# Seven products instead of eight in the Fourier half of an output projection: an encoder layer on one Trainium2 core

## The chip, the cores and the metric

The program runs on one core of one Trainium2 chip. The metric is the device time of the whole program in microseconds (us); before the change the median of three runs is 958.73 us (958.66 to 958.79). All inputs are float32 in HBM and the result is written back to HBM. In the profile PE is TensorE (matmuls and transposes), PEld its weight loads, DVE is VectorE, ACT is ScalarE, POOL is GpSimd, and SP is SyncE, which here issues the DMAs.

## The reference

One layer is applied to a prompt of 256 tokens and a sample of 2048 tokens, width 1024. Cut to what matters:

```python
def encoder_layer(x, w_in, rpb, w_fourier, b_fourier, g_pre, g_na, g_f, w_out, g_post):
    h = rms_norm(x, g_pre)
    proj = h @ w_in
    q, k, v, z_a, u_f, z_f = jnp.split(proj, [...], axis=-1)
    y_a = neighbourhood_attention(q, k, v, rpb)
    y_f = fourier_mix(u_f, w_fourier, b_fourier)
    mixed = jnp.concatenate([rms_norm(y_a, g_na) * jax.nn.silu(z_a),
                             rms_norm(y_f, g_f) * jax.nn.silu(z_f)], axis=-1)
    out = mixed @ w_out
    return x + rms_norm(out, g_post)
```

Both halves of `mixed` are 512 wide. The change concerns the second half: (y_f * silu(z_f)) of 2304 tokens x 512, times the lower 512 rows of `w_out` (512 x 1024, with the gain g_f folded in). The factor of the rms norm is one number per token and is multiplied in when the product leaves PSUM.

## The kernel before

**Stages.** Projections and the Fourier transform fill the first 590 us or so. Then come the attention steps, and at the end the attention half of the output projection (18 tiles of 128 tokens), with the last norm, the residual and the store.

**The attention loop.** There are 36 groups G[k], k = 9 * pr + i: four pairs of heads (pr), and for each the prompt (i = 0) and eight blocks of 256 sample tokens. The loop `for k in range(2, len(G) + 1)` (main loop of the attention, "step k" in this text) works on two groups at once: scores and softmax of G[k], and transposes and value product of G[k-1]. Every engine's order is the order in which the code is written. On PE a step is:

1. `scores(G[k])`: 12 matmuls (L1229, tiles `s`, four PSUM tiles: three of tag "a", which has three buffers, and one of tag "b", which has two).
2. `transp(G[k-1], 0)`: transposes of the first block's softmax weights into `ptb` (L1570). ACT copies one head's half to SBUF (`pt`), DVE the other (L1574).
3. `f_mm(k, range(6))`: six matmuls of the Fourier half (L1497, `po<-wo`, in the page also `po<-w`).
4. `transp(G[k-1], 1)`: the second block, into the same `ptb`, so after the copies of point 2.
5. `f_mm(k, range(6, 12))`: six more matmuls.
6. `pv(G[k-1])`: the value product (L1586), first with the `pt` of block 0, then with that of block 1.

Around them DVE does `bias_max` (L1251, four per step, it reads `s` and writes `w`), the `pt` copies, two reciprocals (L1260) and the product `y` with the gate (L1600). ACT does `exps` (L1256), its `pt` copies and the high part of the next q (`split_q`, L1208). POOL does `soft` (L1263, four per step: it scales the weights `w`, which PE transposes a step later), the low part of q (L1209), the sum of squares `ysq` (L1607), and in steps with i = 5 to 8 the low part of the next pair's k (`split_k`, L1141).

**The Fourier half.** A tile is 128 tokens x 512, laid out as four chunks of 128 (`raw`, loaded by `ys_load`). `ys_mul` multiplies it by the gate on POOL (L1474); `ys_split` makes a high part `yh` (ACT, L1483) and a low part `yl` (DVE, L1488), so that a float32 product becomes three fp32r matmuls per chunk: yh by high weights, yh by low weights, yl by high weights. One half of the output (512 columns) is 4 chunks x 3 = 12 matmuls; a tile has two halves and takes two steps, tile t in steps 2t and 2t + 1. `f_evac` scales a half and writes it to `ofs` (DVE for the first half, L1529; ACT for the second, L1526). The weights lie ready in SBUF as `wo1`.

**Pools and queue.** `gt` hands out 13 buffers of 4 KB per partition (weights `wo1` take eight of them). All DMAs are issued by SP in the written order; each waits for the eighth one before it.

Of the kernel before, what the change touches and what calls it, by code (L numbers as in the profile page):

```python
# [19 lines left out]
D = 1024  # L20
# [154 lines left out]
def build(tc, A, O):  # L175
# [962 lines left out]
    def split_k(kk, x, pool=False):  # L1138
        ts = slice(x * KQ, (x + 1) * KQ)
        (nc.gpsimd.tensor_copy if pool else nc.scalar.copy)(kk[0][:, ts], kk[1][:, ts].bitcast(F32))  # L1140
        nc.gpsimd.tensor_tensor(out=kk[1][:, ts], in0=kk[1][:, ts].bitcast(F32), in1=kk[0][:, ts].bitcast(F32),  # L1141
                                op=ALU.subtract)
# [63 lines left out]
    def split_q(g):  # L1206
        qh, ql = g["qh"], g["ql"]
        nc.scalar.copy(qh, ql.bitcast(F32))  # L1208
        nc.gpsimd.tensor_tensor(out=ql, in0=ql.bitcast(F32), in1=qh.bitcast(F32), op=ALU.subtract)  # L1209
# [228 lines left out]
    gpb = sm.tile([128, D], F32, name="gpb", bufs=1)  # L1438
# [24 lines left out]
    def ys_load(d):  # L1463
# [4 lines left out]
        if half:  # L1468
            d["z"] = sm.tile([128, 4, 128], F32, tag="yz", name="yz", bufs=1)
            nc.sync.dma_start(d["z"], zD[0, :, ts].rearrange("(c p) t -> p c t", p=128))  # L1470
# [5 lines left out]
    def y_parts(d):  # L1476
        d["h"] = sm.tile([128, 4, 128], F32R, tag="yh", name="yh", bufs=3)
        d["l"] = sm.tile([128, 4, 128], F32R, tag="yl", name="yl")
# [6 lines left out]
    def y_lo(d):  # L1485
        if "l" not in d:
            d["l"] = sm.tile([128, 4, 128], F32R, tag="yl", name="yl")
# [15 lines left out]
    def xt_load(d):  # L1503
        d["xt"] = gt([128, D], F32, "xt")
# [8 lines left out]
    def a_mm(d, n, js=range(12)):  # L1513
        if js[0] == 0:
            d["p", n] = ps.tile([128, 512], F32, tag="a" if n else "b", name="po", bufs=3 if n else 2)
        out_mm(d, n, js, d["p", n], lambda n, x, c: WO[x][:, c, n * 512:n * 512 + 512])
# [62 lines left out]
    def pv(g):  # L1579
# [28 lines left out]
        if R is None or hc:  # L1608
            nc.sync.dma_start(yD[0, pr, :, ts], y)

    WO = []

    WK = (24, 26, 28, 29, 31, 32, 33, 34)
    NT = {4: range(2, 4), 8: range(4, 8), 10: range(8, 12), 11: range(12, 16), 12: range(16, 18),
          32: range(4), 34: range(4, 8), 36: range(8, 12)}

# [8 lines left out]
    nc.sync.dma_start(yD[1, 3, :, TP:], Y[:, TP:])  # L1625
    f_mm(0)
# [12 lines left out]
    prep(G[4])  # L1639
    ones32 = sm.tile([128, 32], F32, name="ones32", bufs=1)  # L1640
    nc.vector.memset(ones32, 1.0)
    for k in range(2, len(G) + 1):
# [13 lines left out]
        if k == 9:  # L1656
            nc.sync.dma_start(gpb, pbc(A["gpost"]))
        if k == 23:
            wp = pt.enter_context(tc.tile_pool(name="wp", bufs=1, side="right"))
            WO.extend(wp.tile([128, 4, D], F32R, name="w0%d" % x) for x in range(2))  # L1660
        if k in WK:
            y = WK.index(k)
            nc.sync.dma_start(WO[y % 2][:, y // 2].bitcast(F32), woD[y % 2, y // 2])
        x = k // 2 + 1
        if g:
            scores(g)
            if 2 < k < 34 and k % 2 == 0:
                ys_mul(ftiles[x])
                if x + 1 < 18:
                    ys_load(ftiles[x + 1])  # L1670
            bias_max(g, 0, 0)
            exps(g, 0, 0)
            bias_max(g, 0, 1)
# [4 lines left out]
        if g:  # L1678
# [3 lines left out]
            f_mm(k, range(6))  # L1682
            soft(g, 0)
            exps(g, 1, 1)
        else:
# [3 lines left out]
        if f:  # L1689
            transp(f, 1)  # L1690
        if g:
# [4 lines left out]
            soft(g, 1)  # L1696
            if k == 2:
# [6 lines left out]
        if g:  # L1704
            f_mm(k, range(6, 12))
        else:
            a_mm(atiles[0], 1, range(6))
        if k % 2 and x < 18:
            ys_split(ftiles[x])
        if pr < 3 and i in (5, 6, 7, 8):  # L1710
            split_k(KK[pr + 1], i - 5)
        if k == 34:
            ys_split(atiles[0])
        if g:
# [3 lines left out]
        if f:  # L1718
            pv(f)
        if k + 1 in NT:  # L1720
            norm_sums(sqs if k < 31 else ysq, NT[k + 1])
        if k == 12:
            pq_.close()
        if k + 1 < len(G):
            prep_v(G[k + 1])
        if k + 3 < len(G):
            prep(G[k + 3])
        if k == 28:
            xk = [kp.tile([128, T], F32, tag=x, name="xk") for x in ("kh", "kl")]
        if 32 <= k < 36:  # L1730
            x, d = k - 32, atiles[k - 32]
            d["xt"] = xk[x // 2][:, x % 2 * D:x % 2 * D + D]
            nc.sync.dma_start(d["xt"], A["xn"][d["t"] * 128:d["t"] * 128 + 128, :])
        if k == 32:
            ys_load(atiles[0])
        if k in (34, 35):
            ys_load(atiles[k - 33])
            of_load(atiles[k - 34])

# [112 lines left out]
```

## Time and profile before

| | |
|---|---|
| time, median of three runs | 958.73 us |
| span of the profiled execution, first to last instruction | 957.4 us |
| attention steps 2 to 35 | 606.28 to 846.90 us from the span's start |
| step 36 and the output phase | 846.90 to 957.40 us |
| DVE busy | 707.8 us (74%) |
| ACT busy | 494.8 us (52%) |
| POOL busy | 435.4 us (45%) |

The profiled execution is told by its span; the time of a run has 1.3 us more around it. A busy PE in this profile is a PE with matmuls in flight: one matmul of 512 columns is shown with some 0.39 us, while the next starts 0.23 us after it. So the spacing of starts, not the shown duration, is what a matmul costs on a full PE.

### The profile page before, as it was taken

How to read it: one execution, taken by the hardware profiler on the slowest of the kernel's cores; microseconds unless marked ns; L12 is line 12 of the kernel's file. 1: busy time of each engine (PE TensorE's matmuls, PEld its weight loads, DVE VectorE, ACT ScalarE, POOL GpSimd, SP SyncE). 2: the span in 40 equal slices, each digit the busy share in tenths (PEclk: the TensorE clock that was granted, in tenths of full speed). 3: DMA queues.
4: the chain of work that ended last, by engine and by line, in shares of the span. 5: the costliest groups of instructions: out<-in, count | busy, mean ns of one | idle time of the engine just before them, and what ended most of it. 6: DMA issues, size and time to landing. Idle time of an engine off the chain costs nothing.

```text
span 957.4 us, 16751 instructions
## 1 busy us (share of the span) xinstructions
PE 949.5 (99%) x5625; PEld 790.3 (83%) x5625; DVE 707.8 (74%) x1298; ACT 494.8 (52%) x1068; POOL 435.4 (45%) x411
## 2 busy tenths in 40 slices
PE   9999999999999999999999999999999999999997
PEld 8889988888888888888888779788788888888886
DVE  6758987787975865697887369776666656659997
ACT  6735676423334532233344267677676766644443
POOL 4100002465750302575566055567678686524444
PEclk9999999999999999999999999999999999999998
DMA  9899697557758894499889997788877998989993
GB/s 357 297 383 334 245 343 264 187 193 280 296 190 331 304 342 144 175 345 356 306 297 340 335 329 247 232 241 271 262 241 239 285 301 255 287 289 346 330 346 129
DMA packets 140077, 269.80 MB, mean 282 GB/s; under 512 B 13178, under 2 KB 80464, under 8 KB 136728
## 3 DMA queue, kind: packets, MB, share of 16 engines
q1 hardware_dynamic: 139640, 268.32, 80.5%
q8 instruction: 45, 0.74, 0.3%
q10 hardware_dynamic: 288, 0.40, 0.1%
q14 instruction: 40, 0.33, 0.1%
q0 software_dynamic: 64, 0.02, 0.0%
HBM read 179.00 MB, written 96.81 MB: 288 GB/s over the span
## 4 chain that ended last, share of the span: by engine, by line
PE 98%; DVE 1%; DMA 0%; issue 0%; DVEq 0%
PE po L1497 20%; PE mm L166 18%; PE mm L164 18%; PE mm L165 18%; PE pv L1586 6%; PE ptb L1570 6%; PE s L1229 4%; PE py L164 1%; PE py L165 1%; PE py L166 1%; PE ptb L1043 1%; DMA x<-x 0%; PE pab L1053 0%; PE ppq L1096 0%; PE pz L166 0%; PE pz L164 0%
## 5 line engine op out<-in xcount | busy, mean ns | idle before, releaser
L164 PE MATMUL mm<-xh,wa 128*128 128x512 f32 x448 | 174.4, 389 | 0.0
L165 PE MATMUL mm<-xl,wa 128*128 128x512 f32 x448 | 174.3, 389 | 0.0
L166 PE MATMUL mm<-xh,wa 128*128 128x512 f32 x448 | 174.3, 389 | 0.0
L545 POOL TENSOR_TENSOR ws<-wr 128x512 f32<-128x512 f32 x16 | 23.4, 1465 | 217.8 <-DVE wa L560 127.6
L1263 POOL TENSOR_SCALAR w<-w,m 128x465 f32<-128x465 f32 (+9 forms) x136 | 84.8, 635 | 46.2 <-DVE m L1260 35.5
L166 PEld LDWEIGHTS mm<-xh,wa 128*128 128x128 f32 x448 | 84.1, 188 | 17.6
L164 PEld LDWEIGHTS mm<-xh,wa 128*128 128x128 f32 x448 | 84.1, 188 | 17.5
L165 PEld LDWEIGHTS mm<-xl,wa 128*128 128x128 f32 x448 | 84.1, 188 | 17.4
L1497 PE MATMUL po<-wo,yh 128*128 128x512 f32 x272 | 90.5, 414 | 0.0
L560 DVE TENSOR_TENSOR wa<-wr,wa 128x512 fp32r<-128x512 f32 x60 | 71.8, 1205 | 22.0 <-ACT wa L559 21.8
L1497 PE MATMUL po<-w,yh 128*128 128x512 f32 x280 | 86.8, 391 | 0.0
L1256 ACT ACTIVATE w<-w,m 128x465 f32<-128x465 f32 (+9 forms) x136 | 78.3, 579 | 13.7 <-DVE m L1251 13.3
L1251 DVE CUSTOM_DVE_ANT_1 w<-s,tb 128x465 f32<-128x465 f32 (+8 forms) x124 | 61.2, 531 | 10.1 <-PE s L1229 9.6
L165 PE MATMUL mm<-vl,xh 128*128 128x512 f32 x168 | 65.5, 390 | 0.0
L598 POOL TENSOR_TENSOR mt<-mt,rmask 128x880 f32<-128x880 f32 (+2 forms) x24 | 50.8, 2129 | 32.2 <-DVE mt L594 20.1
L164 PE MATMUL mm<-vh,xh 128*128 128x512 f32 x168 | 65.4, 389 | 0.0
L166 PE MATMUL mm<-vh,xl 128*128 128x512 f32 x168 | 65.4, 389 | 0.0
L1574 DVE COPY pt<-ptb 120x384 f32<-120x384 f32 (+5 forms) x72 | 40.5, 562 | 28.6 <-PE ptb L1570 27.8
L891 DVE TENSOR_TENSOR f<-u,mm 128x512 f32<-128x512 f32 x64 | 43.4, 679 | 24.2 <-PE mm L166 19.7
L1497 PEld LDWEIGHTS po<-w,yh 128*128 128x128 f32 x280 | 52.2, 188 | 10.9 <-issue 0.4
L1570 PE MATMUL ptb<-ident,w 128*120 128x128 f32 (+8 forms) x422 | 58.8, 276 | 0.0
L1586 PEld LDWEIGHTS pv<-pt,v 120*64 120x64 f32 (+9 forms) x880 | 47.4, 136 | 12.9 <-issue 9.7
(287 smaller groups left out, 2369.8 us busy)
## 6 DMA issues: line engine op xcount, KB each, us to landing
wr<-wz SPq DMA_DIRECT2D x48, 512.0 KB
vl<-sD SPq DMA_DIRECT2D x20, 512.0 KB
xm<-xm SPq DMA_DIRECT2D x9, 1024.0 KB
oD<-ofs SPq DMA_DIRECT2D x18, 512.0 KB
of<-oD SPq DMA_DIRECT2D x18, 512.0 KB
yr<-yD SPq DMA_DIRECT2D x34, 256.0 KB
zD<-f SPq DMA_DIRECT2D x16, 512.0 KB
xD<-nx SPq DMA_DIRECT2D x14, 512.0 KB
```

The source lines that it names most:

```text
L164: nc.tensor.matmul(out, lh, rh, start=first, stop=False)
L165: nc.tensor.matmul(out, lh, rl, start=False, stop=False)
L166: nc.tensor.matmul(out, ll, rh, start=False, stop=last)
L560: nc.vector.tensor_tensor(out=o[:, 1], in0=src, in1=o[:, 0].bitcast(F32), op=ALU.subtract)
L598: nc.gpsimd.tensor_tensor(out=o, in0=i, in1=rmask[:, m0:m0 + n].unsqueeze(2).to_broadcast([128, n, 80]), op=ALU.add)
L891: nc.vector.tensor_tensor(out=dst(f, b), in0=src(uu[u]), in1=src(p), op=op)
L1251: nc.vector.tensor_tensor_reduce(out=rows(g["w"][b][:, h, :n], w), in0=rows(g["s"][2 * b + h][:, :nr * sw(w)], sw(w))[:, :, :w], in1=tv, s ...
L1256: nc.scalar.activation(w, w, AF.Exp, bias=m[:, h:h + 1], scale=-1.0, accum_out=m[:, 2 + h:3 + h])
L1263: nc.gpsimd.tensor_scalar(w, w, m[:, 4 + h:5 + h], 1.0, ALU.mult, ALU.mult)
L1497: nc.tensor.matmul(p, (d["l"] if x == 2 else d["h"])[:, c], w(n, int(x == 1), c), start=j == 0, stop=j == 11)
L1570: nc.tensor.transpose(ptb[h][:nk, j * 128:j * 128 + 128], g["w"][b][:, h, c0:c0 + nk], ident)
L1586: nc.tensor.matmul(p[hs, b], g["v"][:nk, v, hs], g["pt"][b][:nk, h, j * 128:j * 128 + 128], start=j == 0, stop=j == len(ch) - 1)
```

## The change

Tiles 8 to 17 are taken in five pairs: pair P with tiles t and t + 1 runs in steps 2t to 2t + 3 (P["k"] = 16, 20, 24, 28, 32). With the first tile's two chunk pairs called A11, A12, the second tile's A21, A22, and the weights cut into B11, B12, B21, B22 (256 x 512 each), the eight products of a pair become seven (Strassen's scheme in Winograd's form):

- sums of the inputs: S1 = A21 + A22, S2 = S1 - A11, S3 = A11 - A21, S4 = A12 - S2
- sums of the weights, made once: T1 = B12 - B11, T2 = B22 - T1, T3 = B22 - B12, T4 = B21 - T2
- products: A11 B11, A12 B21, S2 T2, S1 T1, S3 T3, S4 B22, A22 T4

A product has two chunks, so six matmuls. `p_mm` puts two products into each of a pair's first three steps, at the places of the two `f_mm` blocks, and one into the fourth step. The products of X add up in one PSUM tile (`px`, tag "b") through all four steps; those of Z (`pz`, tag "a", as three of the score tiles) take a new tile each time.

What goes with it:

- **Input sums** (`o_sum`, four of 128 x 256 per pair, POOL), the gate product of the pair's tiles (`o_mul`, POOL), high parts (`o_hi`: two of 128 x 512 on ACT, one on DVE, one of 128 x 256 on ACT) and low parts (`o_lo`: three of 128 x 512 and one of 128 x 256, DVE). Before, a pair of tiles had two high parts (ACT) and two low parts (DVE).
- **Reading out** (`o_out`): eight per pair, two on ACT and six on DVE; before, four per two tiles, two on each.
- **Weight sums**: `t_load` in step 9 loads four pieces of 512 KB, then `t_scale` (ACT), `t_sum` (DVE and POOL), `t_hi` (ACT) and `t_lo` (DVE) run in steps 10 to 16, at the places of the table TS (step, slot). The table AT holds the places of a pair's work (step within the pair, slot).
- **q** is split two steps ahead (`split_q(G[k + 2])`, loads `prep(G[k + 4])`), before one step; in steps 17 and 26 the low part of k goes to DVE.
- The Fourier tiles' norms are taken in steps 6 to 9 (before 8, 10, 11, 12), so that the space of `sqs` can become a pool of seven buffers (`qt`) from step 8 on.
- The weights of the last phase (`WO`) lie in other buffers, `gpb` is loaded in step 34 (before 9), and `xt` of the first four tiles in step 35 and in the first output tile (before in steps 32 to 35).

The core of the diff:

```diff
-    def split_k(kk, x, pool=False):
+    def split_k(kk, x, pool=False, vec=False):
...
-        nc.gpsimd.tensor_tensor(out=kk[1][:, ts], in0=kk[1][:, ts].bitcast(F32), in1=kk[0][:, ts].bitcast(F32),
+        (nc.vector if vec else nc.gpsimd).tensor_tensor(out=kk[1][:, ts], in0=kk[1][:, ts].bitcast(F32), in1=kk[0][:, ts].bitcast(F32),
...
-    NT = {4: range(2, 4), 8: range(4, 8), 10: range(8, 12), 11: range(12, 16), 12: range(16, 18),
+    NT = {4: range(2, 4), 6: range(4, 8), 7: range(8, 12), 8: range(12, 16), 9: range(16, 18),
...
+    def t_load(j):
+        for x in range(2):
+            TR[j, x] = qt([128, D], F32, "wt")
+            nc.sync.dma_start(TR[j, x], A["wo"][1, j + 2 * x])
...
+    def t_lo(j, x, e):
+        src = TR[j, x].rearrange("p (n e) -> p n e", n=2)
+        h, l = TT[j, x]
+        if x:
+            e.tensor_tensor(out=l, in0=src, in1=f_(h), op=ALU.subtract)
+        else:
+            V.scalar_tensor_tensor(out=l[:, 0], in0=src[:, 0], scalar=-1.0, in1=f_(h[:, 0]), op0=ALU.mult,
+                                   op1=ALU.subtract)
+            V.tensor_tensor(out=l[:, 1], in0=src[:, 1], in1=f_(h[:, 1]), op=ALU.subtract)
+
+    TS = ((9, 2, t_load, 0), (9, 6, t_load, 1), (10, 4, t_scale, 0), (11, 3, t_sum, 0, 0, V),
+          (11, 7, t_sum, 0, 1, V), (11, 8, t_scale, 1), (11, 8, t_sum, 0, 2, nc.gpsimd), (12, 2, t_sum, 1, 0, V),
+          (12, 5, t_sum, 0, 3, V), (12, 7, t_sum, 1, 1, nc.gpsimd), (12, 5, t_hi, 0, 0, qt), (12, 6, t_hi, 0, 1, gt),
+          (13, 1, t_lo, 0, 0, V), (13, 4, t_sum, 1, 2, V), (13, 6, t_hi, 1, 0, gt), (13, 8, t_sum, 1, 3, V),
+          (14, 2, t_lo, 1, 0, V), (14, 5, t_lo, 0, 1, V), (14, 7, t_hi, 1, 1, qt), (16, 6, t_lo, 1, 1, V))
...
+    def product(p, a, name, first, cs=range(2)):
+        h, l = a
+        for c in cs:
+            bh, bl = B_(name)[c]
+            for i, (y, b) in enumerate(((h, bh), (h, bl), (l, bh))):
+                nc.tensor.matmul(p, y[:, c], b, start=first and c == i == 0, stop=c == 1 and i == 2,
+                                 skip_group_check=not first)
...
+    AT = (("A3", -1, 8, nc.gpsimd), ("H21", 0, 2, V), ("X2", 2, 3, V), ("M0", -3, 7, nc.gpsimd), ("L4", 2, 0, V),
+          ("X3", 3, 5, V), ("Z1", 1, 7, V), ("L3", 1, 2, V), ("A1", -1, 0, nc.gpsimd), ("X0", 0, 4, nc.scalar),
+          ("A2", -1, 7, nc.gpsimd), ("M1", -2, 8, nc.gpsimd), ("Z0", 0, 8, V), ("X1", 1, 5, nc.scalar),
+          ("L21", 0, 4, V), ("Z1b", 1, 7, V), ("H3", 0, 6, nc.scalar), ("HD", -2, 6, nc.scalar),
+          ("H4", 1, 8, nc.scalar), ("LD", -2, 7, V), ("A4", 0, 7, nc.gpsimd), ("Z2", 2, 7, V))
...
+    PROD = (("X", "D", 0, "11", True), ("Z", "D", 1, "21", True), ("X", "S21", 0, "T2", False), ("Z", "S21", 1, "T1", True),
+            ("X", "S3", 0, "T3", False), ("Z", "S4", 0, "22", True), ("X", "S3", 1, "T4", False))
+
+    def p_mm(P, s, n):
+        if 2 * s + n < 7:
+            p, a, x, b, first = PROD[2 * s + n]
+            if first:
+                P[p] = ps.tile([128, 512], F32, tag="b" if p == "X" else "a", name="p" + p.lower(), bufs=2 if p == "X" else 3)
+            product(P[p], half_of(P[a], x), b, first)
...
-            f_mm(k, range(6))
+            if k < P0:
+                f_mm(k, range(6))
+            side(k, 1)
+            pairs(k, p_mm, 0, 3, 0)
...
-            if k + 1 < len(G):
-                split_q(G[k + 1])
+            if k + 2 < len(G):
+                split_q(G[k + 2])
...
-        if g:
+        if g and k < P0:
             f_mm(k, range(6, 12))
+        elif g:
+            pairs(k, p_mm, 0, 3, 1)
```

In AT the names are: M gate product, A input sum, H high part, L low part (of D, the first tile; S21, which is S2 and S1; S3 with A22; S4), X and Z a read-out of `px` or `pz`. `side(k, slot)` puts the work of TS and AT at ten places of a step, slot 0 after the first `exps`, 1 and 2 on either side of the first `soft`, 4 after the second transposes, 5 after the second `soft`, 6 ahead of the second block of matmuls, 7 and 8 behind it, 9 after `pv`.

Three places show how the order moves. First PE, step 19, the fourth step of the first pair, from the first transposes to the value product; before:

```order
L1570 MATMUL ptb<-ident,w 80x128 x4
L1497 MATMUL po<-wo_5086,yh 128x512 x2
L1497 MATMUL po<-wo_5086,yl 128x512
L1497 MATMUL po<-wo_5087,yh 128x512 x2
L1497 MATMUL po<-wo_5087,yl 128x512
L1570 MATMUL ptb<-ident,w 80x128 x4
L1497 MATMUL po<-wo_5088,yh 128x512 x2
L1497 MATMUL po<-wo_5088,yl 128x512
L1497 MATMUL po<-wo_5089,yh 128x512 x2
L1497 MATMUL po<-wo_5089,yl 128x512
L1586 MATMUL pv<-pt,v 64x128 x8
```

and with the change, the same stretch of PE (`th` and `tl` are the high and low weight sums):

```order
L1573 MATMUL ptb<-ident,w 80x128 x4
L1685 MATMUL px<-th,yh 128x512
L1685 MATMUL px<-tl,yh 128x512
L1685 MATMUL px<-th,yl 128x512
L1685 MATMUL px<-th,yh 128x512
L1685 MATMUL px<-tl,yh 128x512
L1685 MATMUL px<-th,yl 128x512
L1573 MATMUL ptb<-ident,w 80x128 x4
L1589 MATMUL pv<-pt,v 64x128 x8
```

The second block of six matmuls is gone, and `pv` stands right behind the second transposes.

Second DVE, step 14, from the copy of the first transposes to the step's last instruction; before:

```order
L1574 COPY pt<-ptb 120x512
L1251 ISA w,m<-s,tb 128x465
L1251 ISA m 128x1
L1260 RECIPROCAL m<-m 128x2
L1574 COPY pt<-ptb 120x384
L1260 RECIPROCAL m<-m 128x2
L1529 TENSOR_SCALAR ofs<-po,invf 128x512
L1600 TENSOR_TENSOR y<-pv,za 128x2x8x16
```

and with the change (`wt` are the weight sums, `yl` the low part of tile 8):

```order
L1577 COPY pt<-ptb 120x512
L1251 ISA w,m<-s,tb 128x465
L1251 ISA m 128x1
L1260 RECIPROCAL m<-m 128x2
L1663 SCALAR_TENSOR_TENSOR tl<-wt,th 128x512
L1665 TENSOR_TENSOR tl<-wt,th 128x512
L1577 COPY pt<-ptb 120x384
L1260 RECIPROCAL m<-m 128x2
L1661 TENSOR_TENSOR tl<-wt,th 128x1024
L1720 TENSOR_TENSOR yl<-yr,yh 128x512
L1532 TENSOR_SCALAR ofs<-po,invf 128x512
L1603 TENSOR_TENSOR y<-pv,za 128x2x8x16
```

Two instructions now stand ahead of the second copy, and two more ahead of the step's read-out and gate product.

Third POOL, step 14, the whole step; before:

```order
L1263 TENSOR_SCALAR w<-w,m 128x345 x2
L1209 TENSOR_TENSOR ql<-ql,qh 128x256
L1263 TENSOR_SCALAR w<-w,m 128x465 x2
L1141 TENSOR_TENSOR kl<-kl,kh 128x576
L1607 TENSOR_TENSOR ysq<-ysq,sqa 128x2x8x16
```

and with the change:

```order
L1263 TENSOR_SCALAR w<-w,m 128x345 x2
L1209 TENSOR_TENSOR ql<-ql,qh 128x256
L1263 TENSOR_SCALAR w<-w,m 128x465 x2
L1141 TENSOR_TENSOR kl<-kl,kh 128x576
L1702 TENSOR_TENSOR yr<-yr,yz 128x512
L1610 TENSOR_TENSOR ysq<-ysq,sqa 128x2x8x16
L1712 TENSOR_TENSOR ysum<-yr 128x256
```

The gate product of tile 9 and the first input sum have come behind the step's last softmax scaling.

More of the change, by code (lines that the diff above doesn't have):

```diff
@@ new lines, in part, with half_of, src_of, o_mul @@
+    def part(P, name, n):
+        return [sm.tile([128, n, 128], F32R, tag="y%s%d" % (x, n) if n < 4 else "y" + x, name="y" + x,
+                        bufs=3 if n == 4 else 1) for x in "hl"]
+    def half_of(t, x):
+        return [y[:, 2 * x:2 * x + 2] for y in t]
+    def src_of(P, name):
+        if name in ("D", "S3"):
+            return P["d"][name == "S3"]["raw"]
+        return P["S"][:, :4] if name == "S21" else P["S"][:, 4:]
+    def o_mul(P, e, x):
+        d = P["d"][x]
+        e.tensor_tensor(out=d["raw"], in0=d["raw"], in1=d["z"], op=ALU.mult)
+        if x == 0:
+            z_load(P["d"][1])
@@ L1788, in last_tile @@
                 c, x = divmod(j, 3)
[L1789 removed]
+                nc.tensor.matmul(p, (d["l"] if x == 2 else d["h"])[:, c], WO[c][x == 1][:, ns], start=j == 0,
                                  stop=j == 11)
```

178 lines of the change are left out of this document (139 added, 39 removed).

## The prediction

> **What bounds the kernel now.** I read the page's totals first, then its chain of waits, then the timeline of PE inside a step.
>
> ```profile
> PE 949.5 (99%) x5625; PEld 790.3 (83%) x5625; DVE 707.8 (74%) x1298; ACT 494.8 (52%) x1068; POOL 435.4 (45%) x411
> ...
> PE 98%; DVE 1%; DMA 0%; issue 0%; DVEq 0%
> ```
>
> The chain that ended last is 98% PE, so a matmul that goes is worth its spacing unless PE then waits for something. Whether PE waits inside the attention is told by the spacing of starts. Step 15, the part with the two blocks of the Fourier half:
>
> ```profile
> 701.01 0.87 PE L1570 MATMUL ptb<-ident,w 128*120 128x128 f32 x6
> 701.64 0.71 PE L1497 MATMUL po<-wo,yh 128*128 128x512 f32 x2
> 702.19 0.39 PE L1497 MATMUL po<-wo,yl 128*128 128x512 f32 x1
> 702.41 0.63 PE L1497 MATMUL po<-wo,yh 128*128 128x512 f32 x2
> ...
> 703.11 1.03 PE L1570 MATMUL ptb<-ident,w 128*120 128x128 f32 x8
> 703.90 0.70 PE L1497 MATMUL po<-wo,yh 128*128 128x512 f32 x2
> 704.44 0.40 PE L1497 MATMUL po<-wo,yl 128*128 128x512 f32 x1
> 704.67 0.62 PE L1497 MATMUL po<-wo,yh 128*128 128x512 f32 x2
> ...
> 705.46 1.75 PE L1586 MATMUL pv<-pt,v 120*64 120x128 f32 x28
> ```
>
> A matmul of 512 columns takes 0.23 us from start to start (704.44 to 704.67), and no row stands off from its neighbours by more than some 0.1 us, where transposes and output matmuls meet. PE does not wait here; the step is as long as its matmuls.
>
> **What goes: five blocks.** Per pair of tiles 8 x 6 = 48 matmuls become 7 x 6 = 42, so 5 x 6 = 30 go, one block in steps 19, 23, 27, 31 and 35. A block with its two edges reaches from 703.90 to 705.46, 1.56 us. Step 19 itself:
>
> ```profile
> 730.63 0.60 PE L1570 MATMUL ptb<-ident,w 128*80 128x128 f32 x4
> 730.98 0.71 PE L1497 MATMUL po<-wo,yh 128*128 128x512 f32 x2
> ...
> 732.55 1.09 PE L1586 MATMUL pv<-pt,v 80*64 80x128 f32 x16
> ```
>
> 730.98 to 732.55 is 1.57 us. The bare matmuls are 6 x 0.23 = 1.38. No row shows transposes followed straight by `pv`, so the edges may stay: the gain is between 5 x 1.38 = 6.9 and 5 x 1.56 = 7.8 us. I take 7.8, since transposes and `pv` are both plain f32, and the extra tenths stand where f32 meets the output matmuls.
>
> **What comes first in the place of a block.** The block also hid the copy of the second transposes. DVE in step 19:
>
> ```profile
> 731.26 0.42 DVE L1574 COPY pt<-ptb 80x256 f32<-80x256 f32 x1 [0.84 <-PE ptb L1570]
> ```
>
> It ends at 731.68, 0.70 after the place where `pv` would now begin. The first half of `pv` needs only the earlier copy and covers half of its 1.03 us (732.55 to 733.58, the next step's scores), so some 0.2 us of waiting is left in step 19. In the other four the copies are these:
>
> ```profile
> L1574 DVE COPY pt<-ptb 120x384 f32<-120x384 f32 x24 | 13.3, 555 | 6.8 <-PE ptb L1570 6.8
> L1574 DVE COPY pt<-ptb 120x512 f32<-120x512 f32 x16 | 11.1, 691 | 7.8 <-PE ptb L1570 7.3 <-issue 0.5
> ```
>
> With the same 0.28 ahead of a copy, 384 columns are there after 0.84 us and 512 after 0.97; half of `pv` is 0.7 to 0.95 there. That is 0 to 0.3 us each. Taken for the five: 0.8 us. Bounds: nothing, and 7.8, if DVE came as late as the block was long.
>
> **DVE.** Its work per step stands in the table by step (PE, PEld, DVE, ACT, POOL busy):
>
> ```profile
> 684.68:692.17 7.49, 7.49 (x68) 6.14 (x67) 4.70 (x14) 5.33 (x14) 4.10 (x7) 1.00 1.04 331
> 692.17:699.65 7.48, 7.48 (x68) 6.09 (x66) 4.65 (x14) 4.80 (x13) 5.47 (x9) 1.00 0.92 257
> 699.65:707.14 7.49, 7.49 (x68) 6.14 (x66) 4.69 (x14) 5.81 (x15) 5.22 (x7) 1.00 0.52 155
> 707.14:714.39 7.25, 7.25 (x68) 5.98 (x66) 4.32 (x14) 4.53 (x13) 6.91 (x10) 1.00 0.85 273
> 714.39:721.18 6.79, 6.79 (x62) 5.64 (x60) 4.26 (x14) 5.43 (x15) 4.65 (x6) 1.00 0.85 261
> 721.18:727.72 6.54, 6.54 (x63) 5.42 (x62) 3.56 (x14) 3.30 (x12) 6.54 (x10) 1.00 0.88 274
> ```
>
> These are steps 13 to 18. The new kinds of work have rows elsewhere in the program:
>
> ```profile
> L1743 DVE SCALAR_TENSOR_TENSOR of<-po,inva,of 128x512 f32<-128x512 f32 x35 | 25.9, 741 | 1.8 <-PE po L1497 1.7
> L1774 DVE SCALAR_TENSOR_TENSOR xt<-og,sr,xt 128x512 f32<-128x512 f32 x1 | 0.8, 751 | 0.1
> L491 DVE TENSOR_TENSOR vl<-vl,vh 128x1024 fp32r<-128x1024 f32 x16 | 19.0, 1219 | 2.9 <-ACT vh L490 2.9
> 856.91 0.69 DVE L1488 TENSOR_TENSOR yl<-yr,yh 128x512 fp32r<-128x512 f32 x1
> ```
>
> Step 13 gets two of 0.75 and two of 0.69: 4.70 + 2.9 = 7.6 of 7.49 us. Step 14 gets 0.75, 0.69, 1.22 and the low part 0.69: 4.65 + 3.35 = 8.0 of 7.48. So DVE enters step 15 at least 0.6 us late, and nearer 0.9, as some of its waits for PE stay. In step 15 the first copy ended here, and what waits for its end is the second transposes at 703.11:
>
> ```profile
> 702.20 0.55 DVE L1574 COPY pt<-ptb 120x384 f32<-120x384 f32 x1
> ```
>
> That is 702.75, a cover of 0.36 us. So PE waits 0.9 - 0.36 = 0.5 us in step 15 if every instruction takes what it takes alone. It will not; this pair is from the output phase:
>
> ```profile
> 896.99 1.73 DVE L1488 TENSOR_TENSOR yl<-yr,yh 128x512 fp32r<-128x512 f32 x1
> ...
> 895.63 2.54 POOL L1778 TENSOR_TENSOR xt<-of,xt 128x512 f32<-128x512 f32 x2 [2.88 <-PE po L1497]
> ```
>
> The same subtraction as at 856.91, with nothing on POOL, takes 1.73 instead of 0.69 us: POOL's sum ended at 898.17, and 1.73 is the 1.18 us up to there and 0.55 more. One such meeting in steps 13 or 14 adds up to 1.0 us. I take half of it: 1.0 us for step 15 in all, bounds 0 and 2.5. The Trainium skill, "SBUF — State Buffer", section "Who interferes with whom", calls this an exclusive lock: a VectorE instruction with two SBUF inputs and a GpSimd instruction that reads SBUF block each other for a whole instruction. The trace agrees at 896.99; the rule speaks against this change, which adds such work on both sides, and is weighed as a rival below.
>
> From step 16 on a pair adds to DVE three low parts of 0.69 and one of half the size, a copy of 128 x 512 and six read-outs of 0.74, where two low parts and two read-outs were: some 5.5 us in four steps, 1.4 per step on 3.6 to 4.7 busy of 5.8 to 7.5. Only steps 16, 17 (with the low part of k) and 26 come near their length: step 16 is 4.32 + 0.5 + 0.69 + 1.22 = 6.7 of 7.25 us, its old read-out traded for a new one. The copy has no row; between 0.3 and 0.75 us, I take 0.5. For late copies there, and for the third score tile, whose PSUM buffer is now freed by the read-out of `pz`, I take 0.5 us; bounds 0 and 3.
>
> **The rest, costed at nothing.** ACT gets 0.4 us per pair and in steps 10 to 14 up to 1.9 us each on 3.9 to 5.3. The four loads (2 MB) go out when step 9 begins and are first used late in step 10. A pair's operands are made half a step or more before their product. PE's order in the output phase is unchanged, and it still has its loads three to five tiles ahead. If that cover fails, it costs 1 to 3 us at the phase's start.
>
> **The sum.** -7.8 + 0.8 + 1.0 + 0.5 = -5.5 us against the profiled execution, whose span of 957.4 lies 1.3 under the median, as in any run; so 958.7 - 5.5 = **953.2 us**.
>
> The Trainium skill has another price for the matmuls: "TensorE: Matmul & The Clock Gate", section "Back-to-back issue gap", gives about 131 ns per matmul of 512 columns in a sustained stream; 30 of them would be 3.9 us and the sum 957.1. The rows show 0.23 us, and the measurement decides.
>
> **Rivals.**
>
> 1. *No new wait shows.* For it: the averages of DVE and POOL. Against it: step 14's sum over its length. 958.7 - 7.3 (the middle of 6.9 and 7.8) = 951.4 us. Chance 0.15.
> 2. *POOL and DVE block each other and the softmax scaling comes late.* POOL's new work is of these kinds:
>
> ```profile
> L1474 POOL TENSOR_TENSOR yr<-yr,yz 128x512 f32<-128x512 f32 x16 | 20.6, 1290 | 0.0
> L1607 POOL TENSOR_TENSOR ysq<-ysq,sqa 128x256 f32<-128x256 f32 x27 | 19.8, 734 | 22.8 <-ACT sqa L1606 22.8
> L1141 POOL TENSOR_TENSOR kl<-kl,kh 128x576 fp32r<-128x576 f32 x12 | 17.1, 1421 | 0.0
> 736.80 1.09 POOL L1263 TENSOR_SCALAR w<-w,m 128x341 f32<-128x341 f32 x2 [0.20 <-DVE m L1260]
> ```
>
>    In steps 13 to 18 POOL had 32.9 us of work (the table's last busy column); one gate product and five input sums more, one low part of k less make 36.4. DVE's subtractions and sums with both inputs in SBUF are some 11.5 there. Without any overlap that is 47.9 us in 43.0. The scaling has a cover: the row at 736.80 ends at 737.89, and step 21 transposes its result at 741.3, 3.4 us later. So it decides from a lag of some 3.5 us; of a lag of 5 us plus the 1 us that POOL is late anyway, 2.5 reach PE, and as much once more around steps 25 to 28, where the same work meets. 953.2 + 3 = 956 us. By the skill's rule of the lock the time would come out here. Chance 0.18.
> 3. *Slower: the read-out of `pz` stands in front of each next step's third score tile.* One wait in 15 steps, from the point at which DVE enters the end of a step more than a read-out (0.74) late; if two low parts there meet POOL (1.0 each), DVE is 2 us late, the cover of `pv` and the first scores is 2, and the two read-outs stand uncovered: 15 x 0.75 = 11 us. 953.2 + 11 = 964 us. Against it: DVE's average. Chance 0.05.
> 4. *The copies eat the removed blocks* (the change removes matmuls, but not time): `pv` waits as long as a block was, because DVE and POOL, with the step shortened, are late in all five. Up to 7.8 us come back, 958.7 to 960. Against it: in the fourth step DVE has only one read-out. Chance 0.08.
>
> **How the numbers follow.** The forecast, 951.9 to 955, has 0.54. The range leaves out rival 3, rival 4 and the lower part of rival 1: 951.0 to 957.4 us. A measurement of this kernel can tell some 0.2% (1.9 us) from no change. Faster (under 956.8): 0.54 + 0.15 + 0.15 of rival 2 = 0.84; same: the rest of rival 2 and most of rival 4, 0.10; slower: 0.06.
>
> **What would show it.** In the profile after: 30 matmuls less; steps 19, 23, 27, 31 and 35 shorter by 1.3 to 1.5 us each; step 15 longer by some 1.0 us with PE waiting for a `pt` copy of DVE; the other steps of 16 to 35 within 0.2 us of before; the output phase as long as before. Wrong if the steps 14 to 20 together grow by 3 us with PE behind POOL's L1263 (rival 2), or if the scores wait for DVE (rival 3).

## The result and the profile after

The changed kernel takes 967.45 us (median of 5 runs, 962.84 to 968.52); the kernel before took 958.79 beside it. The ratio is 1.0084, with a 95% interval of 1.0067 to 1.0101. It is slower by 8.7 us, where the forecast was 953.2. The profiled execution has a span of 966.7 us against 957.4, so 9.3 us have to be found in it. A run's time lies 1.8 us above its span (968.52 and 966.7 here; 958.80 and 957.0 in a run of the kernel before), not 1.3: that figure set a median beside the span of another execution. In the forecast it cancels. One run among the experiments (a8) went at a granted TensorE clock of 0.65 and took 1342.66 us; it is left out of the medians.

The page of the changed kernel, totals and then the chain that ended last:

```profile
PE 948.1 (98%) x5595; PEld 785.2 (81%) x5595; DVE 738.4 (76%) x1347; ACT 503.3 (52%) x1083; POOL 453.9 (47%) x431
...
DMA 2%; DVE 1%; SPq 0%; issue 0%; ACT 0%; DVEq 0%; ACTq 0%
```

The 30 matmuls are gone (5625 to 5595). The averages still look harmless: POOL is at 47%. But the chain, 98% PE before, is now DMA and DVE, and its shares add up to some 4%: it can be followed back for the last 40 us and no further, and in these it does not run over PE. Where PE waits is told by its list of waits from step 2 on (who waits for whom: us in total, times, longest). Before, this list was empty. Now:

```profile
PE pv L1589 <- DMA v<-vD: 3.7, 3, 1.5
PE pv L1589 <- DVE pt L1577: 1.9, 3, 1.1
PE s L1229 <- DVE ofs L1729: 1.3, 2, 0.9
PE ptb L1573 <- DVE pt L1577: 1.1, 2, 0.7
PE ptb L1573 <- ACT pt L1575: 0.9, 2, 0.5
PE po L1500 <- ACT yh L1486: 0.3, 1, 0.3
```

All six rows are new, and the largest is one the forecast did not have: the value product waits for `v`, a plain load. The table by step shows where (us, then busy time of PE, PEld, DVE, ACT, POOL); steps 14, 16, 17, 19, 20 and 23 of the changed kernel:

```profile
692.14:700.67 8.53, 8.03 (x68) 6.20 (x66) 8.53 (x18) 5.45 (x15) 6.84 (x7) 1.00 0.91 257
708.82:717.55 8.73, 7.66 (x68) 6.17 (x66) 8.19 (x16) 5.58 (x15) 7.13 (x12) 1.00 0.88 285
717.55:725.49 7.94, 7.09 (x63) 5.60 (x62) 7.15 (x19) 5.20 (x15) 7.94 (x9) 1.00 0.66 192
732.16:736.75 4.59, 4.59 (x44) 3.61 (x42) 3.63 (x15) 3.43 (x12) 3.99 (x6) 1.00 0.94 228
736.75:746.00 9.25, 6.65 (x55) 5.15 (x55) 5.29 (x17) 3.84 (x12) 5.30 (x8) 1.00 0.79 268
761.93:769.30 7.37, 6.31 (x62) 5.11 (x60) 4.62 (x15) 4.17 (x12) 3.40 (x5) 1.00 1.02 313
```

and steps 19 and 20 of the kernel before:

```profile
727.72:733.58 5.86, 5.86 (x51) 4.60 (x50) 3.77 (x14) 4.63 (x14) 4.00 (x7) 1.00 0.84 265
733.58:739.90 6.32, 6.32 (x56) 5.16 (x54) 3.96 (x14) 3.56 (x12) 5.36 (x9) 1.00 0.63 205
```

Step 14 was 7.48 us long, 16 was 7.25 and 17 was 6.79. In step 14 DVE is busy to the last (8.53 of 8.53), in 16 nearly so (8.19 of 8.73), and in 17 it is POOL (7.94 of 7.94). Step 19 was 5.86 and is 4.59, near the forecast. Step 20 was 6.32 and is 9.25, and there neither DVE nor POOL is full.

Summed by stage, from the starts of the steps in the profiled executions, in us against the kernel before:

| kernel | steps 14-18 | 19-23 | 24-27 | 28-34 | 35 | output phase | behind PE's end | span |
|---|---|---|---|---|---|---|---|---|
| changed kernel | +4.5 | +2.9 | +1.2 | -1.1 | -1.3 | +1.8 | +1.3 | +9.3 |
| only the weight sums (a4) | +0.3 | 0.0 | 0.0 | 0.0 | 0.0 | +1.1 | +1.4 | +2.1 |
| copy on ACT (a1) | +2.7 | +1.6 | +0.3 | -0.6 | -1.3 | +1.0 | +1.3 | +4.8 |
| z load later (a2) | +5.7 | -2.7 | +3.9 | -1.2 | -1.3 | +2.9 | +1.4 | +9.9 |
| both of these (a3) | +1.8 | -1.7 | +5.4 | -1.2 | -1.3 | +3.1 | +1.3 | +7.2 |
| two z buffers (a6) | +3.3 | -2.6 | -0.3 | -1.2 | -1.3 | +2.6 | +1.3 | +3.1 |
| two z buffers, copy on ACT (a7) | +1.8 | -2.6 | +0.8 | -1.1 | -1.3 | +4.2 | +1.4 | +2.5 |
| a7 with earlier xt (a8) | +2.2 | -2.6 | +2.4 | -1.2 | -1.3 | +3.3 | +1.4 | +3.7 |
| xt three ahead (a9) | +2.2 | +2.0 | +1.3 | -0.7 | -1.3 | 0.0 | +0.2 | +3.6 |
| a7 and xt three ahead (a10) | +1.8 | -2.6 | -0.2 | -1.1 | -1.3 | 0.0 | +0.2 | -3.4 |
| a10 with three low parts moved (a11) | +1.4 | -2.7 | -0.9 | -1.2 | -1.3 | 0.0 | +0.3 | -3.8 |

(Steps up to 13, not shown, differ by 1.3 us at most.) A profile is one execution; the medians stand with the experiments. Two things in the table are not to be read as the edits' doing. Step 14 is 1.05 us longer in the profiles of the changed kernel and of a2, and at most 0.13 longer in the other profiles with pairs, a1 and a9 among them, which have the same code up to there. And in four of the profiles the granted TensorE clock falls to 0.50 for 3.41 us inside the attention, at 744.02 us in a1, 720.00 in a2, 765.71 in a3 and 782.61 in a8. In a1 it lies in step 21 (the column before the last two is the clock):

```profile
744.02:747.43 3.41, 3.41 (x19) 2.71 (x16) 1.90 (x8) 2.50 (x7) 2.86 (x5) 0.50 0.39 115
```

In that profile step 21 is 1.52 us longer although PE waits for nothing there, so some 1.5 us of a1's +1.6 in steps 19 to 23 are the clock. A like part, an estimate, is in steps 14 to 18 of a2 and in steps 24 to 27 of a3 and a8.

Most of the 9.3 us comes from three chains of waits that start on an engine other than PE.

**Chain 1, a copy that does not get in.** The timeline of the changed kernel: DVE in step 16, POOL over the same time, and the same copy in steps 24 and 32 (start, us, engine, line, operation):

```profile
712.22 4.02 DVE L1716 CAST yh<-ysum 128x512 fp32r<-128x512 f32 x1
716.16 0.55 DVE L1577 COPY pt<-ptb 120x384 f32<-120x384 f32 x1
...
711.49 1.43 POOL L1141 TENSOR_TENSOR kl<-kl,kh 128x576 fp32r<-128x576 f32 x1
712.88 0.74 POOL L1712 TENSOR_TENSOR yr<-yr 128x256 f32<-128x256 f32 x1
713.57 0.75 POOL L1610 TENSOR_TENSOR ysq<-ysq,sqa 128x256 f32<-128x256 f32 x1
714.29 0.97 POOL L1263 TENSOR_SCALAR w<-w,m 128x276 f32<-128x276 f32 x2
715.23 0.72 POOL L1209 TENSOR_TENSOR ql<-ql,qh 128x256 fp32r<-128x256 f32 x1
...
773.00 2.84 DVE L1716 CAST yh<-ysum 128x512 fp32r<-128x512 f32 x1
...
775.52 1.47 POOL L1263 TENSOR_SCALAR w<-w,m 128x465 f32<-128x465 f32 x2
...
828.39 0.41 DVE L1716 CAST yh<-ysum 128x512 fp32r<-128x512 f32 x1
```

The high part of S1 and S2 takes 0.41 us in step 32, where POOL is idle until 0.25 us into it, and 4.02 in step 16. There POOL goes from one instruction to the next without a pause until 715.95, and the copy ends 0.29 us after that. In step 24 it gets in earlier: it ends at 775.84, behind three of POOL's instructions, while POOL goes on at once with its scaling from 775.52. In step 16 the `pt` copy behind it is what `pv` waits for (1.07 us), and the read-out of `pz` (L1729) what the next step's scores wait for (0.85 us).

**Chain 2, one z buffer and three queues.** The timeline of the changed kernel again: POOL in step 18, SP's queue from step 17 to 19, and PE in step 20:

```profile
727.46 1.45 POOL L1702 TENSOR_TENSOR yr<-yr,yz 128x512 f32<-128x512 f32 x1
...
722.35 0.41 SPq L1466 DMA_DIRECT2D yr<-yD  x1
728.94 0.36 SPq L1473 DMA_DIRECT2D yz<-zD  x1
729.39 0.94 SPq L1197 DMA_DIRECT2D v<-vP  x2
...
731.40 0.41 SPq L1154 DMA_DIRECT2D tb<-tD  x1
731.90 0.39 SPq L1735 DMA_DIRECT2D oD<-ofs  x1
...
736.13 0.58 SPq L1199 DMA_DIRECT2D v<-vD  x1
...
743.38 1.13 PE L1589 MATMUL pv<-pt,v 128*64 128x128 f32 x16 [1.47 <-DMA v<-vD]
```

and what its list of waits says of the gap behind 722.35:

```profile
SPq L1473 <- POOL yr L1702: 6.1, 1, 6.1
```

`o_mul` of a pair's first tile (L1702) is the last reader of the only `z` buffer, and the load of the second tile's z (L1473) is written right behind it. POOL reaches that product only at 727.46, some 2 us into step 18, so SP stands for 6.1 us at the load, and all that is written behind it stands too. The table of 1200 KB (L1154) goes out at 731.40, at the end of step 18, where it went out 2.5 us into it before, and comes to lie with a store of 512 KB directly ahead of the `v` of step 20. That `v` is issued up to 736.13, and PE has the first of it at 743.38, and the rest later still.

**Chain 3, six buffers for `xt`.** SP's longest waits from step 35 to the end, in the kernel before:

```profile
SPq L1779 <- POOL xt L1778: 41.0, 26, 3.8
SPq L1779 <- POOL xk L1778: 13.1, 8, 5.0
```

and in the changed one:

```profile
SPq L1508 <- DMA yo<-xt: 36.2, 14, 5.4
SPq L1964 <- POOL xt L1963: 12.8, 11, 3.8
```

Before, SP waited for POOL's sums, to store them. Now it waits 14 times at `xt_load` (L1508) for a store out of `xt`: the load four tiles ahead gets the buffer of the tile two before, whose result is still on its way out. Behind it in SP's queue stand the `yr` loads of the coming tiles; the last part of the changed kernel's chain of waits (start, us, what) reads so:

```profile
934.10 5.91 DMA yr<-yD
940.10 4.71 DMA yo<-xt
944.87 0.33 SPq L1508
...
946.24 4.63 DMA yr<-yD
950.95 0.63 ACT yh L1486
951.60 0.06 DVE yl L1491
```

Load, store, issue of the next loads, load: PE is at the end of this chain and no longer its cause.

### The profile page after: what moved, and what is told of

The parts are those of the page before. It is cut to its first block, busy times and chain, and to the rows that moved or that the text cites. A ratio compares the mean times of both kernels' runs of the same rounds, so it can differ in the third digit from the quotient of the medians.

```text
span 966.7 us, 16758 instructions
## 1 busy us (share of the span) xinstructions
PE 948.1 (98%) x5595; PEld 785.2 (81%) x5595; DVE 738.4 (76%) x1347; ACT 503.3 (52%) x1083; POOL 453.9 (47%) x431
## 5 line engine op out<-in xcount | busy, mean ns | idle before, releaser
L1263 POOL TENSOR_SCALAR w<-w,m 128x465 f32<-128x465 f32 (+9 forms) x136 | 91.0, 681 | 30.6 <-DVE m L1260 20.6
L1500 PE MATMUL po<-wk,yh 128*128 128x512 f32 x280 | 87.2, 393 | 0.3 <-ACT yh L1486 0.3
L1963 POOL TENSOR_TENSOR xt<-of,xt 128x512 f32<-128x512 f32 x34 | 43.2, 1291 | 54.5 <-issue 32.9
L1589 PE MATMUL pv<-pt,v 120*64 120x128 f32 (+9 forms) x880 | 58.4, 278 | 5.5 <-DMA v<-vD 3.7
L1500 PEld LDWEIGHTS po<-wk,yh 128*128 128x128 f32 x280 | 52.0, 188 | 11.7 <-ACT yh L1486 1.0
```

The lines of the kernel that those rows point to most:

```text
L1263: nc.gpsimd.tensor_scalar(w, w, m[:, 4 + h:5 + h], 1.0, ALU.mult, ALU.mult)
L1500: nc.tensor.matmul(p, (d["l"] if x == 2 else d["h"])[:, c], w(n, int(x == 1), c), start=j == 0, stop=j == 11)
L1589: nc.tensor.matmul(p[hs, b], g["v"][:nk, v, hs], g["pt"][b][:nk, h, j * 128:j * 128 + 128], start=j == 0, stop=j == len(ch) - 1)
```

## The experiments

All but one start from the changed kernel. The times are medians, the ratios those to the kernel before in the same set of runs, with their 95% intervals.

**First set: where does the lag start?** The theory at this point was that the starved copy starts it and SP's queue carries it. One rival: POOL has too much work of its own.

The copy on ACT:

```diff
-    AT = (("A3", -1, 8, nc.gpsimd), ("H21", 0, 2, V), ...
+    AT = (("A3", -1, 8, nc.gpsimd), ("H21", 0, 2, nc.scalar), ...
```

> One edit: the high part of a pair's S1 and S2 (a copy of 128 x 512, once per pair) is made by ACT instead of DVE. Theory 1 (the copy on DVE, 4.02, 2.84 and 1.27 us in steps 16, 24 and 28 beside a POOL that never pauses, is what makes DVE late, and with it POOL's softmax scaling and gate product, and with these the z load on which SP's queue stands): the waits of PE in steps 16 and 17 (1.27 and 1.10), in 20 and 23 (2.96 and 1.22) and most of those in 22 to 27 go, about 8 of the 12 us; steps 14 and 15 keep theirs, the output phase too: 960 us. Theory 2 (POOL has too much work of its own, the copy is a victim): only steps 16 and 17 get shorter, by 2 us, the v waits in 20 and 23 stay: 965 to 966 us.

965.63 us, 1.0069 (1.0053 to 1.0086). Steps 14 and 16 are as long as before again (+0.1 and 0.0 us). Only step 16 can be the edit's doing: the copy first runs there, and step 14 is one of the two things said under the table. Step 17 is still 1.8 us longer, and the wait for `v` in step 20 is there with 2.3 us; the one in step 23 is gone. So the copy costs what it costs on the spot, and it is not what makes SP stand at the z load: that is as the rival would have it. The runs of a1 (964.02 to 966.30) lie within the spread of the changed kernel's (962.84 to 968.52), so 1.8 us between the medians are not clear of noise.

The z load at the end of its step, behind the loads of `v`:

```diff
-        if x == 0:
-            z_load(P["d"][1])
...
             prep(G[k + 4])
+        pairs(k, lambda P, s: z_load(P["d"][1]), -3, -3)
```

> One edit: the load of the second tile's z, which must wait until POOL has used the first tile's z, is issued at the end of its step, behind the loads of v, za and q for the following steps, instead of ahead of them. If SP's queue standing at that load is what makes v late, the waits for v in steps 20 and 23 (4.2 us together) go: 963 us; then DVE's and POOL's lag, which those stops had let them catch up, may show as other waits, and 965 is the upper end. If v is late for another reason (the DMA engines are full, or the ring of eight transfers is), they stay: 967 us.

967.06 us, 1.008 (1.0056 to 1.0105). The waits for `v` go (stage 19-23 from +2.9 to -2.7), and as much comes up in step 24, 3.4 us longer. Its waits of PE name a new releaser:

```profile
PE pv L1589 <- DVE pt L1577: 2.7, 3, 1.1
PE ptb L1573 <- POOL w L1263: 1.6, 1, 1.6
```

The transposes now wait for the softmax scaling. The second tile's z was issued at 760.84, in step 23, and POOL stood 5.4 us at the second gate product until 765.82, with the scaling queued behind it. (The profile names a store as the releaser there; the z load had landed only at 765.7, and the store is not what the product reads.) The same chain, entered at another link. With both edits:

> Both edits: the copy on ACT and the z load behind the loads of v. Theory 1 with SP's queue as its carrier: hardly better than the copy alone, 959 to 960 us. Two separate causes: 960 to 961 us here, with the copy alone at 964 or more. What should be left by either is 1.3 us in steps 14 and 15 and 3.1 us from the output phase, against 6.5 us gained in the five shortened steps: 958.8 - 6.5 + 1.7 + 3.1 = 957.1 at best.

966.96 us, 1.0077 (1.005 to 1.0104): both expectations fall. The copy's stage gets better (+1.8), and step 24 worse by 4.1 us: PE waits 2.5 us for POOL's L1263 there, and most of the rest, an estimate, is the stretch at half clock. The two edits together gave nothing in the median: the later z load had only moved its wait to step 24. So what ties that load to the gate product, the one buffer, had to be tried.

Only the weight sums, with the old twelve matmuls per half for all tiles (the sums are made and not read):

```diff
-    P0 = 16
+    P0 = 36
```

> The weight sums are made in steps 9 to 16 as in the changed kernel, q is split two steps ahead and the output phase has its changed buffers, but no pair uses Strassen's products: tiles 8 to 17 are computed with twelve matmuls per half as before (the sums are never read). Shows what the preparation and the moved loads cost by themselves. If the waits in steps 14 and 15 come from the weight sums: these two steps stay 1.0 and 0.6 us longer than before and so does the output phase by 3.1 us, nothing else: 958.8 + 1.7 + 3.1 = 963.6 us. If the lag of DVE and POOL in steps 16 to 23 also starts in the weight sums: over 965 us. If the output phase is longer only because of the pairs: 960.5 us.

962.87 us, 1.0037 (1.002 to 1.0054). In the attention almost nothing is left: no wait of PE, steps 19 to 35 as before within 0.01 us, step 18 longer by 0.25, and steps 14 and 15 not longer at all. So the sums alone do not make PE wait; it takes the pairs' work beside them. But the output phase is longer, with no pair in it. Of the 8.7 us some 4 are therefore the price of the changed buffers and loads of that phase, and have nothing to do with the products.

**Second set: one buffer, and the output phase.** A z buffer of 2 KB for the second tile, beside `qt`'s seven buffers, loaded with the raw tile:

```diff
-    def z_load(d):
+    def z_load(d, pool=None):
...
-        if x == 0:
-            z_load(P["d"][1])
...
                 ys_load(P["d"][1], False)
+                z_load(P["d"][1], gz)
...
+            gz = pt.enter_context(tc.tile_pool(name="gz", bufs=1, side="right"))
```

> One edit to the changed kernel: the second tile of a pair has a z buffer of its own (2 KB per partition beside the seven buffers of qt), and its z is loaded together with its raw tile, so its load waits for no gate product any more, SP's queue does not stand at it, and POOL does not wait for it before the second gate product. Theory 2 (one z buffer ties SP, POOL and DMA into a chain): the waits for v in steps 20 and 23, and those for POOL's L1263 in step 24 that came with the later z load, go and nothing takes their place; what the copy on DVE and the waits of steps 14 to 17 cost stays: 967.5 - 4.2 = 963 us. If DVE's and POOL's own work is the bound (theory 3), the lag stays and PE waits elsewhere: 965 to 967 us.

963.19 us, 1.005 (1.0035 to 1.0065), as expected: 4.3 us less, and no wait for `v` or for L1263. The copy on DVE still takes 3.33 us in step 16. With it on ACT as well:

> Two z buffers, and the high part of S1 and S2 on ACT. Theory 2: waits are left only in steps 15 and 17 (0.7 and 0.9 to 1.8 us) and in 25 to 27 (1 to 2 us), some 3.5 us against 6.5 us gained, and the output phase is longer as with the sums alone (+4): 958.8 - 6.5 + 3.5 + 4 = 959.8 us. Theory 3: 963 us or more.

960.34 us, 1.0019 (1.0009 to 1.003), as expected, 2.9 us less than with the second buffer alone. Theory 3, that DVE and POOL have too much work, falls: in a6 both have all the work of the changed kernel, in a7 DVE has only the five copies less, and PE's waits in the attention add up to 2.9 us in a7, where they were 8.9 in the changed kernel:

```profile
PE ptb L1573 <- DVE pt L1577: 1.4, 1, 1.4
...
PE ptb L1573 <- ACT pt L1575: 0.9, 2, 0.5
PE s L1229 <- DVE ofs L1727: 0.6, 1, 0.6
```

Then the output phase. The theory was bytes: less of `xt` is there when the phase begins. Once with the loads one step earlier, once from the other side, with the kernel before and its `xt` loads as late as in the changed kernel:

```diff
-        if k == 35:
-            xt_load(atiles[0])
-            xt_load(atiles[1])
+        if k in (34, 35):
+            xt_load(atiles[2 * k - 68])
+            xt_load(atiles[2 * k - 67])
...
-                xt_load(atiles[x])
+                if x > 3:
+                    xt_load(atiles[x])
```

> As the run before it, and the xt loads of the first four tiles go out one step earlier (0 and 1 at the end of step 34, 2 and 3 at the end of step 35) instead of at the end of step 35 and in the first output tile. If the output phase is longer because 2 MB less are there when it begins and its transfers then run at the DMA engines' limit, about 1 MB (some 3 us at 330 GB/s) comes back: 2 to 3 us less than the run before it. If the phase waits for something else: the same time.

> The kernel before, with one edit: the xt loads of the first four tiles go out where the changed kernel has them (tiles 0 and 1 at the end of step 35, 2 and 3 in the first output tile), into the buffers that they had. If these loads are what makes the output phase of the changed kernel longer: +3 to +5 us, all of it behind step 36, 962 to 964 us, with runs that differ by more than 1 us as those of the sums alone do. If it is the other moved loads (weights, gpb) or the pairs: 958.8 us.

959.48 us, 1.0012 (0.9999 to 1.0025), where a7 had 960.34, and 958.78 us for the kernel before with late loads (958.77 without), ratio 0.9999 (0.9989 to 1.0008). The second is clear: late `xt` loads alone cost the kernel before nothing. The first decides little: 0.9 us less lies between the two expectations, and its nine runs go from 957.87 to 962.85. Its profile still has SP's 14 waits for a store out of `xt` (36.6 us), and an output phase 0.9 us shorter than that of a7. So at most a part of the cost can be bytes. The profile's SP waits (chain 3 above) then gave the next theory, the buffers.

**Third set: `xt` three tiles ahead.**

```diff
         for x in range(2, 5) if j == 0 else (j + 4,):
             if x < 18:
                 of_load(atiles[x])
-                xt_load(atiles[x])
+            if 2 < x < 19:
+                xt_load(atiles[x - 1])
```

> One edit to the changed kernel: in the output phase a tile's xt is loaded three tiles ahead instead of four (of stays four ahead). In the changed kernel the load four tiles ahead takes the buffer (six are left of qt's seven) from which the tile two before is still being stored, and SP's queue stands at it 14 times, 36 us in all, with the loads of yr behind it. If that makes the output phase longer: the phase is as long as before again (111.8 to 112.2 us from the start of step 35 becomes about 109.5), the waits in the attention stay: 967.5 - 3.5 = 964 us. If it is the number of bytes left for the phase: 967 us.

960.93 us, 1.0026 (1.0014 to 1.0039). The output phase is as long as before to 0.01 us, and what stands behind PE's end too (+0.2). The median fell by 6.5 us and not by 3.5; in the profile, 2.9 of 5.7 us are from that phase, and the rest from steps 14 to 23, which vary from execution to execution: in step 16 the copy took 1.64 us here and the step is as long as before, where 4.02 us went with +1.5 in the changed kernel and 3.33 with +0.8 in a6. Together with the two edits of the second set:

> Three edits: two z buffers, the high part of S1 and S2 on ACT, xt three tiles ahead. If the three causes add up, 960.3 (the first two) less the output phase's 3 to 3.5 us: 957 us, the first version below the kernel before. If the output phase has another cause: 960 us.

956.30 us, 0.9972 (0.9962 to 0.9983): faster than the kernel before by 2.6 us (958.91 beside it). From step 35 on SP's longest wait is again the one for POOL's sums:

```profile
SPq L1964 <- POOL xt L1963: 50.7, 34, 3.8
```

and PE's list of waits from step 2 on has three rows left:

```profile
PE ptb L1573 <- ACT pt L1575: 0.9, 2, 0.5
PE s L1229 <- DVE ofs L1727: 0.6, 1, 0.6
PE ptb L1573 <- DVE pt L1577: 0.4, 1, 0.4
```

What was left came from subtractions ahead of DVE's urgent work. The timeline of a7, DVE and POOL at the beginning of step 26:

```profile
776.69 2.25 DVE L1718 TENSOR_TENSOR yl<-ysum,yh 128x256 fp32r<-128x256 f32 x1
...
776.54 1.42 POOL L1141 TENSOR_TENSOR kl<-kl,kh 128x576 fp32r<-128x576 f32 x1
777.91 0.75 POOL L1610 TENSOR_TENSOR ysq<-ysq,sqa 128x256 f32<-128x256 f32 x1
```

The low part of S4 waits through two POOL instructions, ahead of three of the step's four `bias_max`. So three low parts move to places where DVE is idle:

```diff
-           (14, 2, t_lo, 1, 0, V), (14, 5, t_lo, 0, 1, V), (14, 7, t_hi, 1, 1, qt), (16, 6, t_lo, 1, 1, V))
+           (14, 2, t_lo, 1, 0, V), (14, 7, t_hi, 1, 1, qt), (15, 5, t_lo, 0, 1, V), (15, 8, t_lo, 1, 1, V))
...
-    ... ("X2", 2, 3, V), ("M0", -3, 7, nc.gpsimd), ("L4", 2, 0, V),
+    ... ("L4", 2, 2, V), ("X2", 2, 3, V), ("M0", -3, 7, nc.gpsimd),
```

> As the run before it, and three of DVE's subtractions move to places where DVE is idle: the low part of S4 from the start of its step to behind the first copies, two low parts of weight sums from steps 14 and 16 to the end of step 15. The waits left in steps 15, 17 and 26 (0.7, 0.9 and 1.6 us) go if DVE's place in the step decides: 957 - 2.5 = 954.5 us. If POOL's and DVE's blocking simply moves with them: 957 us.

955.34 us, 0.9964 (0.995 to 0.9978), 1.0 us less where 2.5 were expected, and not clear of noise, as the runs overlap (954.58 to 957.08, a10 955.65 to 957.95). The waits in steps 15, 17 and 26 are gone, and this is all that is left from step 2 on:

```profile
PE ptb L1573 <- ACT pt L1575: 1.3, 2, 1.1
```

Nearly all of it (1.1 us) is in step 18, a new wait: there `bias_max` waits 1.1 us for POOL's mask of the next table (L1158, 2.06 us), which POOL reaches late, and ACT's copy stands behind it.

## Why the prediction was wrong

The forecast was 953.2 us, and its range ended at 957.4. With three causes taken away (one z buffer, the copy on DVE, the `xt` loads four tiles ahead) the kernel takes 956.30 us. Of these the sum had sized one far too low, had one among the terms costed at nothing, and did not have the third.

**What goes** was right. The five steps are shorter by 1.2 to 1.4 us each where nothing else touches them (19, 31 and 35 in the changed kernel: 1.26, 1.20, 1.32; step 23 in a10: 1.39; 27 has 0.4 of waiting for ACT's `pt` copy and 0.77 left). That is some 6 us, where 7.8 - 0.8 was forecast.

**The copy** is the first term that was mis-sized. The forecast had "between 0.3 and 0.75 us, I take 0.5"; it measured 0.41 to 4.02. The bound for such meetings, "up to 1.0 us", came from a pair of rows with a single POOL instruction. In step 16 POOL went through six without a gap, and DVE waited for the end of the last; in steps 20, 28 and 24 it got in behind one, two and three. The Trainium skill, "SBUF — State Buffer", section "Who interferes with whom", counts copies that run in a two-port mode among those that take the lock, and speaks of blocking for a whole instruction; the rows agree that the copy is blocked, and show that it can be blocked for six instructions. Moved to ACT it was worth 2.9 us beside two z buffers; alone it gave 1.8, within the spread of the runs.

**"The rest, costed at nothing"** holds the second. That PE "still has its loads three to five tiles ahead" was read from the places in the program. It held for the places, not for the buffers: a load is only ahead if its buffer is free. The range given for a failure, 1 to 3 us, was about right in the profile (3.1), low for the medians (4.0 between a7 and a10), and stood in no sum.

**SP's queue** is missing altogether. The z load of the second tile was a moved step with a DMA, put behind a POOL instruction whose tile holds the only buffer; the forecast counted POOL's work there, but did not ask what is queued behind that load on SP (the `v` of the steps that follow), nor what behind the second gate product on POOL (the scaling). 4.3 us went with a second buffer.

**DVE in steps 13 to 15** was right in its place: 1.0 us was forecast for step 15, and it is 0.66 us longer in the changed kernel, 0.66 to 1.20 in the other profiles with pairs but for a11, where two low parts are moved and nothing is left. But PE waits there for ACT's `pt` copy (L1575, 0.48 us), not for DVE's: ACT's work ahead of it stood for DVE's late `y` (L1603) and began 2.2 us into the step, where it began 0.6 us into it before. The forecast did not have the 1.05 us of step 14. There the z load landed some 1 us later in the step than in a1, and the gate product ran beside a subtraction of weight sums on DVE that took 1.58 us, where it took 0.72 in a1; that came in two profiles of ten.

**The rivals.** Rival 2 (POOL and DVE block each other and the scaling comes late, 956 us) had the blocking right, but let the lag reach PE only through the scaling, and so came to 3 us. In the changed kernel it came through `pt`, the `pz` read-out and SP; the scaling shows up in a2 and a3 alone. Rival 3 had the `pz` read-out in 15 steps; it was late in two (1.3 us). Rival 4 did not come: the shortened steps without other waits kept their gain. Two figures of the working are off and changed nothing: rival 2 counts five input sums in steps 13 to 18 where the kernel makes four, and by its own rows a pair adds some 4.5 us to DVE and not 5.5. A slower kernel had a chance of 0.06, for one mechanism that hardly showed; three others did it together. Their sizes depend on which of the others are there: taken away in the order z, copy, `xt` they gave 4.3, 2.9 and 4.0 us; alone, the copy gave 1.8 and `xt` 6.5.

Left open is how much of the spread from run to run in the changed kernel (5.7 us, against 0.7 for the one before) belongs to which chain, and how much to stretches at half clock; with all three gone it was 2.3 us. Whether the copy on DVE at a place where POOL pauses would do as well as on ACT was not tried.

## What to carry to other kernels

When a change moves loads and buffers as well as arithmetic, write down for every in-order queue, SP's and POOL's too, what each new wait stands in front of: a load that waits for a late consumer delays every load behind it. "So many tiles ahead" means nothing until the buffers are counted against the time from load to the last store out of them. And when an edit removes a wait and as much comes up elsewhere, look for what both waits hang on; here it was a buffer of 2 KB.

## What the runs showed of the hardware

A copy from SBUF to SBUF on DVE (128 x 512) took 0.41 us in step 32 of the changed kernel, where POOL came only 0.25 us into it. It took 4.02, 0.74, 2.84 and 1.27 us in steps 16, 20, 24 and 28, where POOL ran without a pause. Each of these four ended about 0.3 us after one of POOL's instructions, the sixth, first, third and second that it met (716.24 after 715.95, 740.57 after 740.28, 775.84 after 775.53, 802.62 after 802.33). Only in step 16 was that the last of POOL's row. Subtractions of two SBUF inputs differ in the same way: one of 128 x 256 in a7 took 2.25 us over two instructions (778.94 after 778.66), while one of 128 x 512 in step 14 of the changed kernel ended at 698.21 with POOL running on. So the price of such a meeting can be several of the other engine's instructions, up to six here, and not only one; what lets DVE in between two of them is not shown.

The granted TensorE clock fell to 0.50 for 3.41 us inside the attention in four of the thirteen profiles, each time during a wait of PE or within 1.2 us behind one (the waits were 0.9 to 2.5 us long). The changed kernel's PE waited 1.5 and 1.1 us in step 20 without it, so a wait does not always bring it.
